# Loading the last row tile of the first x in nine transfers of 64, 14, 2, 12, 4, 10, 6, 8 and 8 partitions instead of seventeen, most of them of five

## The chip, the cores and the metric

The kernel runs on one core of a Trainium2 chip. The metric is the device time in microseconds of one execution; lower is better. Before the change the median is 514.57 us (514.47 to 514.59, 4 runs). "Faster" and "slower" mean by over 2%. In the views PE is TensorE (matmuls), DVE VectorE, ACT ScalarE, POOL GpSimd and SPq the queue of the sync engine; a packet is one record of a DMA engine's work, and a transfer lands when its data has arrived.

## The reference

```
x: (32, 512, 1024) float32     weight: (32, 1024, 768) float32
out = np.matmul(x, weight)     (32, 512, 768) float32
```

Thirty-two independent matrix products. The core must read 168 MB and write 50 MB.

## The kernel before

Weights and x come in through GpSimd's DMA queue, cast to bf16 on the way. The first x alone comes uncast through the sync queue: three row tiles in one transfer, the fourth ("x_fourth", called one_sb in the profile) in pieces:

```
x_first = x_pool.tile([P, MT - 1, K], F32, name="x_sb")
x_fourth = one_pool.tile([P, 1, K], F32, name="one_sb")
nc.sync.dma_start(x_first, x_view[0, :, :MT - 1])
few = [slice(at, first + 20, 4) for first in (0, 20, 40) for at in range(first, first + 4)]
for rows in (slice(64, 96), slice(96, 112), slice(112, P), slice(60, 62), slice(62, 64), *few):
    nc.sync.dma_start(x_fourth[rows, 0], x_view[0, rows, MT - 1])
load_w(0)
```

One partition's row of this tile is 4 KB; "a row" below means one of these. Nothing before the third matmul group of batch 0 needs the tile. At the end of the kernel the sync queue carries the last stores:

```
nc.sync.dma_start(out_view[b - 1, :, halves[0]], outs[b - 1][:, halves[0]])
for late in range(B - LATE, B - 2):
    nc.sync.dma_start(out_view[late], outs[late])
nc.sync.dma_start(out_view[b - 1, :, halves[1]], outs[b - 1][:, halves[1]])
# ... cut: matmuls of the last batch, which issue its two half stores from the sync queue
```

Of the kernel before, what the change touches and what calls it, by code (L numbers as in the profile page):

```python
# [13 lines left out]
def kernel(  # L14
# [9 lines left out]
    P = 128  # L24
# [29 lines left out]
    def banks():  # L54
        return [mpsum.tile([P, 512], F32, name=f"pm{i}") for i in range(3)]

    def load_pair(b):

        xs[b] = x_pool.tile([P, 2 * MT, K], BF16, name="x_sb")
        nc.gpsimd.dma_start(out=xs[b], in_=pair_view[b // 2])  # L60

    def load_last():
        xs[B - 1] = x_pool.tile([P, MT, K], BF16, name="x_sb")
        nc.gpsimd.dma_start(out=xs[B - 1], in_=x_view[B - 1])  # L64

    def load_w(b):
        ws[b] = w_pool.tile([P, KT, N], BF16, name="w_sb")
        at = 0
        for n in CHUNKED.get(b, (KT,)):
            nc.gpsimd.dma_start(out=ws[b][:, at:at + n, :], in_=w_view[b, :, at:at + n, :])  # L70
            at += n
# [9 lines left out]
    def transpose_pair(b, mt):  # L81

        both = xT_pool.tile([P, 2, JT, P // 2, 2, 2], BF16, name="xT")
        for half in range(2):
            nc.vector.tensor_copy(  # L85
                both[:, :, :, :, half, :].rearrange("p b j i r -> p j b i r"),
                words(b, mt + MT * half).rearrange("p j (b i r) -> p j b i r", b=2, r=2),
            )
        return [both[:, r].rearrange("p j i h r -> p j (i h) r") for r in range(2)]

    def transpose_last(mt):
        xT = xT_pool.tile([P, JT, P, 2], BF16, name="xT")
        nc.vector.tensor_copy(  # L93
            xT.rearrange("p j m r -> p (j m r)"), words(B - 1, mt).rearrange("p j m -> p (j m)")
        )
        return xT

    def transpose_first(mt):

        xT = xT_pool.tile([P, JT, P, 2], BF16, name="xT")  # L100
        rows = x_first[:, mt] if mt < MT - 1 else x_fourth[:, 0]
        for h in range(2):
            pt = tpsum.tile([P, JT, P], F32, name="pt")
            for i in range(JT):
                nc.tensor.transpose(pt[:, i, :], rows[:, JT * h + i::KT], ident)  # L105
            nc.vector.tensor_copy(  # L106
                xT[:, 2 * h:2 * h + 2].rearrange("p j m r -> p j r m"),
                pt.rearrange("p (j r) m -> p j r m", r=2),
            )
        return xT  # L110
# [8 lines left out]
    def matmuls(pm, half, xT, b, kos, together):  # L119
        for ko in kos:  # L120
            for i, (bank, at, off, size) in enumerate(SPLITS[half]):
                shares = half == 1 and i == 0
                nc.tensor.matmul(  # L123
                    pm[bank][:, at:at + size],
                    xT[:, ko // 2, :, ko % 2],
                    ws[b][:, ko, off:off + size],
                    start=(ko == 0 and not (together and shares)),
                    stop=(ko == KT - 1),
                    skip_group_check=together,
                )  # L130

    def open_out(b):

        if b == B - 2:
            outs[b] = one_pool.tile([P, MT * N], F32, name="one_sb")
            return
        if b % 2 == 0 or b == B - 1:
            twos[b // 2] = out_pool.tile([P, 2, MT * N], F32, name="out_sb")
        outs[b] = twos[b // 2][:, b % 2]

    def evacuate(b, pair, pm):
        o = outs[b][:, pair * N2:(pair + 1) * N2]
        nc.scalar.copy(o[:, 0:512], pm[0])  # L143
        nc.vector.tensor_copy(o[:, 512:1024], pm[1])  # L144
        nc.scalar.copy(o[:, 1024:N2], pm[2])  # L145

    with tc.manual_schedule():

        x_first = x_pool.tile([P, MT - 1, K], F32, name="x_sb")
        x_fourth = one_pool.tile([P, 1, K], F32, name="one_sb")  # L150
        nc.sync.dma_start(x_first, x_view[0, :, :MT - 1])  # L151
        few = [slice(at, first + 20, 4) for first in (0, 20, 40) for at in range(first, first + 4)]
        for rows in (slice(64, 96), slice(96, 112), slice(112, P), slice(60, 62), slice(62, 64), *few):
            nc.sync.dma_start(x_fourth[rows, 0], x_view[0, rows, MT - 1])
        load_w(0)
        ident = const.tile([P, P], F32)
        make_identity(nc, ident)
        load_pair(1)
        load_w(1)
        load_w(2)  # L160
        load_pair(3)

        def store(at):
            nc.gpsimd.dma_start(out=two_view[at], in_=twos[at])  # L164

        ready = {}
        for b in range(B):
            if b % 2 and b + AHEAD + 1 < B:
                if b + AHEAD + 1 == B - 1:
                    load_last()  # L170
                else:
                    load_pair(b + AHEAD + 1)
            if b % 2 and 2 < b < B - HELD - AHEAD:
                store((b - 3) // 2)
            if b + AHEAD < B:
                load_w(b + AHEAD)
            if b == B - LATE:
                store(b // 2 - 2)
                store(b // 2 - 1)
            if b == B - 1:  # L180
                halves = [slice(pair * N2, (pair + 1) * N2) for pair in range(2)]
# [4 lines that stand above are left out]
            open_out(b)  # L186
            if b == 0:
                xT = {mt: transpose_first(mt) for mt in range(MT - 1)}
            elif b == B - 1:
                xT = {mt: transpose_last(mt) for mt in range(MT)}  # L190
            else:
                if b % 2:
                    for mt in range(MT):
                        ready[b, mt], ready[b + 1, mt] = transpose_pair(b, mt)
                xT = {mt: ready.pop((b, mt)) for mt in range(MT)}
            if b not in CHUNKED:
                for pair in range(2):
                    pm = banks()
                    for half in range(2):
                        mt = 2 * pair + half  # L200
                        if mt not in xT:
                            xT[mt] = transpose_first(mt)
                        matmuls(pm, half, xT[mt], b, range(KT), False)
                    evacuate(b, pair, pm)
                continue
            pms = [banks() for _ in range(2)]
            at = 0
            for n in CHUNKED[b]:
                last = at + n == KT
                for mt in range(MT):  # L210
                    matmuls(pms[mt // 2], mt % 2, xT[mt], b, range(at, at + n), True)
                    if last and mt % 2 == 1:
                        pair = mt // 2
                        evacuate(b, pair, pms[pair])
                        if b == B - 1:
                            nc.sync.dma_start(out_view[b, :, halves[pair]], outs[b][:, halves[pair]])
                at += n
# [30 lines left out]
```

## Time and profile before

| | before |
|---|---|
| time, median | 514.57 us |
| span in the profile | 512.7 us |
| TensorE busy | 435.4 us (85%) |
| memory traffic | 218.1 MB, 425 GB/s |
| x_fourth used from | 42.9 us |
| TensorE's waits for weights | 26.2 us |

Two more lines matter. The first is the group of the main matmuls from the page: busy time and mean duration behind the first bar, the idle time before them and its main cause behind the second. The second is the queue row of the sync engine's transfers, with packets, bytes and share:

```profile
L123 PE MATMUL pm<-w_sb,xT 128*128 128x256 bf16 (+1 forms) x2048 | 353.7, 336 | 26.4 <-DMA w_sb<-in_weight_dram 26.2
q1 hardware_dynamic: 1248, 8.39, 4.1%
```

Below the views lie the packet records of the trace: start, duration, bytes and queue of every DMA packet. They carry no engine number. But every transfer ends with a four-byte completion packet on each engine it used, so a weight load leaves sixteen of them, and an engine's lag against the others can be followed from load to load. Where this text says "the packet records", it means that.

### The profile page before, as it was taken

Reading aid. Unit: us, or ns where it says so; the run is one execution under the profiler, and the core shown is the slowest. Engines: PE = TensorE matmul, PEld = TensorE weight load, DVE = VectorE, ACT = ScalarE, POOL = GpSimd, SP = SyncE. Lnnn points to the kernel's source line nnn. Section 1 sums busy time; section 2 is a strip of 40 time slices with the busy share of each in tenths; the row PEclk is TensorE's granted clock in tenths of the full one; section 3 lists DMA queues with packets and bytes.
Section 4 is the critical chain, followed back from the end, with each engine's and each line's share of the span. In section 5 each row is a group of like instructions: output and inputs, shape, how many; then the busy total and the mean of one; then the engine's idle time right before and its main releaser. Section 6 shows DMA issues by size and latency. Waiting matters only on the chain.

```text
span 512.7 us, 5785 instructions
## 1 busy us (share of the span) xinstructions
PE 435.4 (85%) x2576; PEld 278.7 (54%) x2576; DVE 130.0 (25%) x196; ACT 76.1 (15%) x129; POOL 39.1 (8%) x73
## 2 busy tenths in 40 slices
PE   1806999999999996997989989798898989999991
PEld 1504666666666663654646546464464645666660
DVE  0202324141515141320413205041040410514121
ACT  1100121212121201111111111111101111120201
POOL 3000010101010101001010000101001000010000
PEclk9956999999999998997999989899798998999997
DMA  8999999999999999999999999999999999999998
GB/s 240 224 221 213 218 220 216 333 221 310 243 218 336 215 324 231 228 325 220 330 223 234 318 223 334 217 247 304 221 333 218 258 295 220 331 215 212 320 427 345
DMA packets 12712, 135.63 MB, mean 265 GB/s; under 512 B 1296, under 2 KB 1296, under 8 KB 3088
## 3 DMA queue, kind: packets, MB, share of 16 engines
q0 software_dynamic: 11440, 126.88, 96.6%
q1 hardware_dynamic: 1248, 8.39, 4.1%
q8 instruction: 20, 0.33, 0.2%
q14 instruction: 4, 0.03, 0.0%
HBM read 167.77 MB, written 50.33 MB: 425 GB/s over the span
## 4 chain that ended last, share of the span: by engine, by line
PE 46%; DMA 37%; issue 8%; DVE 5%; another core or an unknown queue 1%; POOL 1%; ACT 0%; SPq 0%; POOLq 0%
PE pm L123 40%; DMA w_sb<-in_weight_dram 28%; DMA one_sb<-in_x_dram 8%; PE pt L78 5%; DVE xT L85 4%; DVE out_sb L144 1%; POOL out_dram L164 0%; PE pt L105 0%; POOL w_sb L70 0%; POOL x_sb L60 0%; DVE one_sb L144 0%; DVE xT L93 0%; ACT out_sb L145 0%; SPq L151 0%
## 5 line engine op out<-in xcount | busy, mean ns | idle before, releaser
L123 PE MATMUL pm<-w_sb,xT 128*128 128x256 bf16 (+1 forms) x2048 | 353.7, 336 | 26.4 <-DMA w_sb<-in_weight_dram 26.2
L123 PEld LDWEIGHTS <-xT 128*128 128x128 bf16 x2048 | 205.3, 101 | 170.3 <-DMA w_sb<-in_weight_dram 29.3
L144 DVE COPY out_sb<-pm 128x512 f32<-128x512 f32 x62 | 42.9, 691 | 317.6 <-PE pm L123 317.6
L78 PE MATMUL pt<-ident,x_sb 128*128 128x128 f32 x496 | 79.8, 302 | 10.5 <-DVE xT L85 10.2
L78 PEld LDWEIGHTS pt<-ident,x_sb 128*128 128x128 f32 x496 | 69.3, 209 | 21.5 <-DVE xT L85 18.7
L85 DVE COPY xT<-pt 128x1024 bf16<-128x1024 bf16 x120 | 77.4, 687 | 11.0 <-PE pt L78 11.0
L143 ACT COPY out_sb<-pm 128x512 f32<-128x512 f32 x62 | 36.3, 585 | 271.7 <-PE pm L123 271.7
L145 ACT COPY out_sb<-pm 128x512 f32<-128x512 f32 x62 | 36.3, 585 | 145.7 <-PE pm L123 145.6
L70 POOL DMA_DIRECT2D w_sb<-in_weight_dram x37 | 20.1, 544 | 404.8 <-PE pm L123 397.6
L105 PE MATMUL pt<-ident,one_sb 128*128 128x128 f32 x8 | 1.9, 421 | 19.1 <-DMA one_sb<-in_x_dram 19.1
L106 DVE CAST xT<-pt 128x512 bf16<-128x512 f32 x8 | 5.8, 733 | 34.6 <-PE pt L105 34.1
L105 PE MATMUL pt<-ident,x_sb 128*128 128x128 f32 x24 | 5.3, 383 | 10.5 <-DMA x_sb<-in_x_dram 10.3
L105 PEld LDWEIGHTS pt<-ident,one_sb 128*128 128x128 f32 x8 | 1.6, 219 | 19.4 <-issue 19.4
L164 POOL DMA_DIRECT2D out_dram<-out_sb x14 | 10.1, 719 | 6.7 <-ACT out_sb L143 3.5
L105 PEld LDWEIGHTS pt<-ident,x_sb 128*128 128x128 f32 x24 | 4.1, 209 | 11.5 <-issue 10.3
L60 POOL DMA_DIRECT2D x_sb<-in_x_dram x15 | 8.1, 539 | 10.9 <-DMA w_sb<-in_weight_dram 10.9
L144 DVE COPY one_sb<-pm 128x512 f32<-128x512 f32 x2 | 1.4, 690 | 9.0 <-PE pm L123 9.0
L93 DVE COPY xT<-pt 128x1024 bf16<-128x1024 bf16 x4 | 2.6, 686 | 0.2 <-PE pt L78 0.2
L143 ACT COPY one_sb<-pm 128x512 f32<-128x512 f32 x2 | 1.2, 585 | 6.4 <-PE pm L123 6.4
L145 ACT COPY one_sb<-pm 128x512 f32<-128x512 f32 x2 | 1.2, 585 | 1.6 <-PE pm L123 1.6
L143 ACT ACT_TABLE_LOAD x1 | 1.3, 1283 | 0.7 <-PEq L232 0.7
L64 POOL DMA_DIRECT2D x_sb<-in_x_dram x1 | 0.5, 528 | 2.1 <-DMA w_sb<-in_weight_dram 2.1
(6 smaller groups left out, 0.9 us busy)
## 6 DMA issues: line engine op xcount, KB each, us to landing
w_sb<-in_weight_dram POOLq DMA_DIRECT2D x28, 1536.0 KB, 41.7
out_dram<-out_sb POOLq DMA_DIRECT2D x14, 3072.0 KB, 55.3
x_sb<-in_x_dram POOLq DMA_DIRECT2D x15, 2048.0 KB, 49.8
w_sb<-in_weight_dram POOLq DMA_DIRECT2D x7, 768.0 KB, 38.2
out_dram<-out_sb SPq DMA_DIRECT2D x2, 1536.0 KB
x_sb<-in_x_dram SPq DMA_DIRECT2D x1, 1536.0 KB
out_dram<-one_sb SPq DMA_DIRECT2D x2, 768.0 KB
out_dram<-out_sb SPq DMA_DIRECT2D x2, 768.0 KB
```

The lines of the kernel that those rows point to most:

```text
L60: nc.gpsimd.dma_start(out=xs[b], in_=pair_view[b // 2])
L70: nc.gpsimd.dma_start(out=ws[b][:, at:at + n, :], in_=w_view[b, :, at:at + n, :])
L78: nc.tensor.transpose(pt[:, j, :], pairs[:, mo, j::JT], ident)
L85: nc.vector.tensor_copy(both[:, :, :, :, half, :].rearrange("p b j i r -> p j b i r"), words(b, mt + MT * half).rearrange("p j (b i r) -> ...
L93: nc.vector.tensor_copy(xT.rearrange("p j m r -> p (j m r)"), words(B - 1, mt).rearrange("p j m -> p (j m)"))
L105: nc.tensor.transpose(pt[:, i, :], rows[:, JT * h + i::KT], ident)
L106: nc.vector.tensor_copy(xT[:, 2 * h:2 * h + 2].rearrange("p j m r -> p j r m"), pt.rearrange("p (j r) m -> p j r m", r=2),)
L123: nc.tensor.matmul(pm[bank][:, at:at + size], xT[:, ko // 2, :, ko % 2], ws[b][:, ko, off:off + size], start=(ko == 0 and not (together an ...
L143: nc.scalar.copy(o[:, 0:512], pm[0])
L144: nc.vector.tensor_copy(o[:, 512:1024], pm[1])
L145: nc.scalar.copy(o[:, 1024:N2], pm[2])
L164: nc.gpsimd.dma_start(out=two_view[at], in_=twos[at])
```

## The change

The intent, as the code shows it: fewer issues, an earlier landing, and the extra rows spread as a ramp over 14 engines instead of piled on five.

```
-        few = [slice(at, first + 20, 4) for first in (0, 20, 40) for at in range(first, first + 4)]
-        for rows in (slice(64, 96), slice(96, 112), slice(112, P), slice(60, 62), slice(62, 64), *few):
+        ramp = []
+        for at, n in enumerate((14, 12, 10, 8)):
+            ramp += [slice(at, at + 4 * n, 4), slice(at + 4 * n, 64, 4)]
+        for rows in (slice(64, P), *ramp):
             nc.sync.dma_start(x_fourth[rows, 0], x_view[0, rows, MT - 1])
```

Nothing else differs.

## The prediction

> **What bounds the kernel now.** I read the head of the page first, then the chain of waits in order of time, then the DMA view of the last 23 us, and at last the trace's DMA packet records (start, duration, bytes, queue) one by one.
>
> The page says that the 16 DMA engines are busy from the second slice to the last, and the memory line says at what rate:
>
> ```profile
> PE   1806999999999996997989989798898989999991
> DMA  8999999999999999999999999999999999999998
> HBM read 167.77 MB, written 50.33 MB: 425 GB/s over the span
> PE 46%; DMA 37%; issue 8%; DVE 5%; another core or an unknown queue 1%; POOL 1%; ACT 0%; SPq 0%; POOLq 0%
> ```
>
> The reader is to see that PE has gaps and DMA has none. 218.1 MB in 512.7 us is all that the kernel does; TensorE is busy 435 us and fits beside it. The chain names PE for 46%, but a chain only follows the last waits. So I looked where the changed transfer stands in it, and at what happens to the gained time:
>
> ```profile
> 1.18 12.13 DMA one_sb<-in_x_dram
> 13.33 15.00 DMA one_sb<-in_x_dram
> 28.35 14.36 DMA one_sb<-in_x_dram
> 42.90 1.94 PE pt L105 x8
> ...
> 155.40 46.68 DMA w_sb<-in_weight_dram
> ...
> 373.89 49.68 DMA w_sb<-in_weight_dram
> 423.62 6.40 PE pm L123 x28
> ```
>
> The fourth row tile of the first x lands at 42.4 us and lets PE go on at 42.9. PE then runs nearly without a gap (101.3 us busy of the 104 between 43 and 147), and from 147 on it waits for weights. A lead won at 43 is therefore handed to waits for weights after 147. The end itself:
>
> ```profile
> 486.86 0.39 SPq L182 DMA_DIRECT2D out_dram<-one_sb  x1
> 487.30 2.31 SPq L184 DMA_DIRECT2D out_dram<-out_sb  x2
> 489.72 1.11 SPq L185 DMA_DIRECT2D out_dram<-one_sb  x1
> 501.16 1.63 SPq L216 DMA_DIRECT2D out_dram<-out_sb  x2
> ```
>
> The last two stores are issued from 501.2 to 502.8. In the packet records the stores ahead of them end only at 505.6 to 507.4, and the last half store completes between 509.33 and 511.41, engine by engine. A backlog of stores stands between PE's end and the kernel's end, some 3 us deep. **The end is the finish of the slowest DMA engine.** The DMA view of 490 to 513 us (40 slices of 0.575 us) shows the engines running out one after the other at its right end:
>
> ```profile
> DMA  8999999998999899989998999899999998842000
> ```
>
> **How unequal the engines are.** Every weight, x and store transfer from GpSimd ends with 16 four-byte completion packets, one per engine. The time between the completions of two successive weight loads is the same on most engines (7.276 us, 8 packets of 0.907 us), so an engine's lag stays until something is added to it, and I can follow each one. Three kinds appear:
> - Five engines take the twelve transfers of five rows. Between 14.4 and 41 us they fall back by 2.06 us against the rest, 0.17 us for each row with its completion packet; two of them take two rows more and stand at about 2.45 us of lag at 50 us, the other three at 2.2 us.
> - Eight others are hit by the instruction queue: 20 packets of 16384 bytes, 0.9 us each, come in turn to these eight and cost each time about 1.1 us. Four get three, four get two.
> - Three get neither.
>
> The final completions, from the first engine, are 0, 0.17, 0.23 (the three with neither), then 0.80 to 1.21, and at the end 1.65, 1.74, 1.76, 1.85, 2.02 and 2.08 us. The last, 2.08, is an instruction engine with three hits. So are all or nearly all of the six late ones; I can't exclude that one at 1.85 or 2.02 is of the five. The mean is 1.14: perfect balance would gain only 0.94 us, 0.18% of the time. That caps the gain.
>
> **What the Trainium skill says.** "DMA: Bandwidth & Descriptors", section "Why a DMA increments its semaphore by 16 and not by 1": a transfer from the sync queue runs on the largest number of engines, up to 16, that divides its row count, and on the lowest-numbered ones. The trace agrees: the first x and the seventeen pieces leave 128 completion packets, 4 x 16 + 2 x 2 + 12 x 5. The same page, "Queues, rings and completion order": each engine takes turns between its queues, packet by packet. It agrees: in the 5-row stage a small row or a completion packet alternates with a 12288-byte weight packet, a pair every 1.98 us. "Runtime: NRT & Kernel Launch", "Instruction fetch mechanics": instructions are refilled in 16 KiB blocks by a queue of their own; the 20 packets of 16384 bytes fit it. No view names an engine, so which numbers the eight have is my assumption: 8 to 15, as 0 to 4 carry the fives.
>
> **The change part by part.** Rows per engine, from the rule above. Before: three 16-engine transfers give 2+1+1 = 4 to all; two pairs give 2 to engines 0 and 1; the fives give 12 to engines 0 to 4. That is 18 on 0 and 1, 16 on 2 to 4, 4 on 5 to 15 (sum 128). After: the 64 rows give 4 to all; 14, 2, 12, 4, 10, 6, 8, 8 give 8 more to engines 0 and 1, 7 to 2 and 3, 6 to 4 and 5, 5 to 6 and 7, 3 to 8 and 9, 2 to 10 and 11, 1 to 12 and 13, none to 14 and 15. Totals 12, 11, 10, 9, 7, 6, 5, 4 for each pair (sum 128). At 0.17 us a row:
> - engines 0 to 4: 5 or 6 rows fewer, 0.85 to 1.0 us earlier. Mostly not on the end.
> - engines 5 to 7: 5 or 6 more, 0.85 to 1.0 us later, from about 0.1 to about 1.1. Off the end.
> - engines 8 to 15: 3, 3, 2, 2, 1, 1, 0, 0 more, up to 0.5 us later. **These set the end.** Only two completion packets of 4 ns fall away there.
> - Transfers: 17 issues become 9, about 8 x 0.66 us less on the sync queue, which has nothing else to do until 487 us. Worth nothing at the end.
> - Landing of the tile: engine 0 had 14 row-and-completion pairs after the large pieces (14.9 to 42.4 us, 1.96 each). It will have eight after the 64 rows (which should end near 14): four at 2.59 us beside the x pair, four at 1.98, so near 32 us, an estimate. PE goes on 10 us sooner, and waits 10 us more for weights later. DMA order is unchanged, and the queue is never empty in between, so the end does not move by it.
>
> Sum: 0 for PE's lead, 0 for issues, and for the end the last of the eight. If the instruction hits begin at engine 8, the one at 2.08 is engine 10 and gets 2 rows: +0.33. Averaged over the other possible starts the later maximum rises by about 0.2 to 0.25. I take +0.2: 514.55 + 0.2 = **514.75 us**.
>
> **The rivals.**
> 1. PE's ten early microseconds count. For it: the chain gives the small tile 8% and PE is in the chain from 424 to 502. Against it: between them PE waited for weights, in pieces of 47 and 50 us in the chain, which come at the DMA's pace, and after PE's end 3 us of backlog remain. If it were right: up to 504.5 us.
> 2. The balance gains: one of the five engines is truly the last, or the eight don't lie where I think, so that the late ones get no rows. For it: a late engine whose lag grows by 0.07 us each time a store passes seems to be one of the five. Against it: it is at most second. Taking it away alone leaves 2.08, so the gain is under 0.1 us: 514.45 to 514.55. The whole balance would make 513.6.
> 3. The instruction fetches come at other times as PE runs earlier, and hit other packets. Single hits cost from 0.93 to 1.32 us in the records, so 0.2 us either way.
> 4. More rows on more engines slow the weights near the start and PE starves. Against it: the same 0.5 MB of the tile moves in both, and the weights' packets keep 0.907 us beside it.
>
> **Range and chances.** From +0.5 (three rows on the slowest engine) and 0.2 of fetch luck, 515.2 at the top; from -0.1 (rival 2) and 0.15 of luck, 514.3 below. The three runs of before lie within 0.11 us, so noise adds little. A change of 2% would be 10 us, eleven times the whole imbalance; only rival 1 comes near, and not over it: faster 0.004, slower 0.004.
>
> **What would show it.** The fourth tile's transposes (line 105, one_sb) start near 32 instead of 42.9; PE's waits for weights grow by about as much; the DMA row stays at nine and the rate at 425 GB/s; the spread of the last completions loses its three early engines but keeps its last one. I am wrong if the last completions move by over half a microsecond, if the last stores no longer queue behind others, or if the eight late engines turn out to be those that lost rows.

## The result, and the profile after

The changed kernel takes **515.12 us** (median of 4 runs, 514.92 to 515.23) against 514.57 (514.47 to 514.59). The ratio is 1.0011, with an interval of 0.9993 to 1.0028: the same, by the 2% rule. Ratios here are the mean time of one kernel's fast runs over that of the other's of the same rounds, so they are not quite the ratio of the medians. Still, all nine timed runs of the changed kernel (four here, five below) are slower than every run of the kernel before beside them, so the half microsecond is real.

The beginning of the chain of waits after the change (start, length, what) shows the earlier landing:

```profile
1.20 14.03 DMA one_sb<-in_x_dram
15.24 15.25 DMA one_sb<-in_x_dram
30.69 1.94 PE pt L105 x8
```

Its matmul group and queue row, which answer to the two quoted of before:

```profile
L123 PE MATMUL pm<-w_sb,xT 128*128 128x256 bf16 (+1 forms) x2000 | 355.0, 337 | 38.4 <-DMA w_sb<-in_weight_dram 35.9
q1 hardware_dynamic: 1216, 8.39, 4.1%
```

Where the lead went shows in windows of 31 to 43, 43 to 147 and 147 to 424 us (length, then busy time and count of each engine, the granted TensorE clock, DMA share, GB/s), before first:

```profile
31.00:43.00 12.00, 0.10 (x1) 0.13 (x2) 0.00 (x0) 0.00 (x0) 0.00 (x0) 0.50 1.04 225
43.00:147.00 104.00, 101.29 (x615) 66.46 (x616) 32.44 (x49) 16.97 (x29) 9.24 (x16) 0.98 1.02 246
147.00:424.00 277.00, 244.65 (x1427) 154.58 (x1426) 71.27 (x108) 42.14 (x72) 20.82 (x37) 0.94 1.02 267
```

```profile
31.00:43.00 12.00, 11.28 (x60) 8.13 (x60) 7.12 (x11) 0.59 (x1) 0.53 (x1) 0.81 1.03 218
43.00:147.00 104.00, 95.52 (x575) 61.22 (x585) 26.03 (x40) 17.58 (x30) 8.71 (x15) 0.98 1.02 246
147.00:424.00 277.00, 240.60 (x1375) 152.36 (x1399) 70.59 (x107) 41.04 (x70) 20.85 (x37) 0.93 1.02 267
```

TensorE does 11.2 us more in the first window, then 5.8 and 4.0 us less in the next two, while DMA moves the same: 246 and 267 GB/s in both kernels. TensorE starts on the tile 12.2 us earlier (42.90 to 30.69) and waits 9.7 us more for weights (26.2 to 35.9). The lead was handed back. (The record lacks 48 of the matmuls, so the idle time is good to a microsecond or two.) The 32 fewer packets of the sync queue, with the same bytes, are the completion packets of eight fewer transfers: 16 + 16 + 2 + 2 + 12 x 5 + 16 = 112 before, 16 + 14 + 2 + 12 + 4 + 10 + 6 + 8 + 8 = 80 after. That agrees with the rule of how many engines a transfer uses (quoted in the prediction), for 14, 12 and 10 too.

The end is where the two kernels differ. These are the sync queue's last issues after the change, then the DMA view of both kernels from 508 to 513 us, before first. It has 40 slices of 0.125 us; a digit is the mean busy share of the 16 engines in tenths:

```profile
488.06 0.36 SPq L184 DMA_DIRECT2D out_dram<-one_sb  x1
488.46 1.72 SPq L186 DMA_DIRECT2D out_dram<-out_sb  x2
490.66 0.43 SPq L187 DMA_DIRECT2D out_dram<-one_sb  x1
502.36 1.63 SPq L218 DMA_DIRECT2D out_dram<-out_sb  x2
```

```profile
DMA  9899798988888878835534231100000000000000
GB/s 442 344 442 492 295 442 344 442 344 344 344 344 344 344 295 344 344 148 246 246 148 197 98 147 49 49 0 0 0 0 0 0 0 0 0 0 0 0 0 0
```

```profile
DMA  9998978875575754542423132222310100000000
GB/s 393 393 393 344 393 295 344 344 295 246 246 295 246 295 246 197 246 197 98 197 98 148 49 147 98 98 98 98 147 49 0 49 0 0 0 0 0 0 0 0
```

Before, the row stays at 0.7 or more up to the 17th slice and is over nine slices (1.1 us) later. After, it falls to 0.5 at the 10th slice, and a few engines go on alone to the 32nd. By the packet records the engines complete the store ahead of the last two only between 504.6 and 508.4 us, after the last issues began, so there is still a queue and TensorE's end does not set the time. The bytes are the same; why the engines run out less evenly is what the experiments are for.

### The profile page after: what moved, and what is told of

The parts are those of the page before. It is cut to its first block, busy times and chain, and to the rows that moved or that the text cites. A ratio compares the mean times of both kernels' runs of the same rounds, so it can differ in the third digit from the quotient of the medians.

```text
span 513.4 us, 5729 instructions
## 1 busy us (share of the span) xinstructions
PE 436.8 (85%) x2528; PEld 279.6 (54%) x2576; DVE 129.9 (25%) x196; ACT 76.3 (15%) x129; POOL 39.1 (8%) x73
## 4 chain that ended last, share of the span: by engine, by line
PE 49%; DMA 34%; issue 5%; DVE 5%; another core or an unknown queue 3%; POOL 1%; ACT 0%; SPq 0%; POOLq 0%
PE pm L123 44%; DMA w_sb<-in_weight_dram 28%; DMA one_sb<-in_x_dram 6%; PE pt L78 5%; DVE xT L85 4%; DVE out_sb L144 1%; PE pt L105 0%; POOL out_dram L166 0%; POOL w_sb L70 0%; POOL x_sb L60 0%; DVE one_sb L144 0%; DVE xT L93 0%; ACT out_sb L145 0%; SPq L151 0%
## 5 line engine op out<-in xcount | busy, mean ns | idle before, releaser
L123 PE MATMUL pm<-w_sb,xT 128*128 128x256 bf16 (+1 forms) x2000 | 355.0, 337 | 38.4 <-DMA w_sb<-in_weight_dram 35.9
L144 DVE COPY out_sb<-pm 128x512 f32<-128x512 f32 x62 | 42.9, 692 | 330.6 <-PE pm L123 330.6
L143 ACT COPY out_sb<-pm 128x512 f32<-128x512 f32 x62 | 36.3, 586 | 284.2 <-PE pm L123 284.2
L145 ACT COPY out_sb<-pm 128x512 f32<-128x512 f32 x62 | 36.3, 586 | 134.4 <-PE pm L123 134.2
L105 PEld LDWEIGHTS pt<-ident,x_sb 128*128 128x128 f32 x24 | 4.2, 211 | 11.2 <-issue 10.2
```

The lines of the kernel that those rows point to most:

```text
L105: nc.tensor.transpose(pt[:, i, :], rows[:, JT * h + i::KT], ident)
L123: nc.tensor.matmul(pm[bank][:, at:at + size], xT[:, ko // 2, :, ko % 2], ws[b][:, ko, off:off + size], start=(ko == 0 and not (together an ...
L143: nc.scalar.copy(o[:, 0:512], pm[0])
L144: nc.vector.tensor_copy(o[:, 512:1024], pm[1])
L145: nc.scalar.copy(o[:, 1024:N2], pm[2])
```

## The experiments

The theory: the time is the finish of the slowest DMA engine. An engine's finish is its equal share of the main traffic, plus 0.17 us for each extra row of x_fourth, plus about 1.1 us for each 16 KB instruction packet that falls on it. The rival reasons are the early landing (TensorE runs ahead and triggers things elsewhere), the single front transfer, the number of odd transfers, and chance.

First, whom the instruction packets hit. In the changed kernel the transfers are nested: only engines 0 to 13 have a completion of the 14-row transfer, only 0 to 11 one of the 12-row transfer, and so on. So the packet records now give each engine's number up to a pair, and engines 4 and 5 are told apart by the fives of the kernel before, which reach 4 only. The eight engines that take the 16 KB packets are, in their turn: **5**, one of 6 and 7, one of 8 and 9, 10 and 11, 12 and 13, and one of 14 and 15. The order of the durations in a turn also tells where the turn begins. The first turn of three traces:

```
before   892 893 938 945 936 967 974 961 ns
after    893 893 948 944 921 975 974 962 ns
sixes    893 893 948 945 936 974 974 961 ns
```

Twenty packets over eight engines give three to the first four of the turn. The prediction had assumed engines 8 to 15. A second assignment of the packets, with every engine held to the same 715 packets of GpSimd's queue, gave the same eight, and in the changed kernel's first trace it gave each engine exactly the rows of the rule. The four with three hits ended there as follows (us), in the order of the turn:

```
rows added   before   after    later by
    6        510.97   512.12   1.15   (engine 5)
    5        511.08   511.85   0.77
    3        511.40   511.81   0.41
    2        511.35   511.74   0.39
```

All four are later, and the more rows an engine got, the later it is. This is one trace of each kernel; the last completion of the other four traces of the changed kernel is up to 0.4 us later still.

**Ten sixes: engine 5 alone.** In the kernel before, the twelve fives become ten transfers of six rows.

```
-        few = [slice(at, first + 20, 4) for first in (0, 20, 40) for at in range(first, first + 4)]
+        few = [slice(at, first + 24, 4) for first in (0, 24) for at in range(first, first + 4)]
+        few += [slice(48, 60, 2), slice(49, 60, 2)]
```

> Ten transfers of six rows in place of twelve of five: engine 5 gets ten rows more, engines 0 to 4 two fewer, nothing else changes. Theory (engine 5 takes three of the instruction fetches and is among the late ones, as the residues in the trace after say): it finishes 10 x 0.17 = 1.7 us later, the end 1.3 to 1.45 us later: 515.85 to 516.05. Rival, which is the prediction's assumption (the fetches are on engines 8 to 15, engine 5 is one of the three that finish first): engine 5 gets from about 0.1 to 1.8 us and the end stays: 514.5 to 514.65.

Measured: 516.05 us median (515.61 to 516.12, 5 runs) against 514.84 for the kernel before on that chip, which was less quiet (514.46 to 515.47, 9 runs). That is 1.2 us more by the medians and 1.15 by the lowest runs. The DMA view of 508 to 513 us, slices of 0.125 us:

```profile
DMA  9899995987959875715333031101010101101000
GB/s 492 344 442 393 442 393 246 393 344 295 442 246 442 344 295 246 295 49 246 147 147 147 0 147 49 49 0 49 0 49 0 49 0 49 49 0 49 0 0 0
```

From the 27th slice on a single engine is at work: 49 GB/s is one packet of 6144 bytes in a slice, and one comes every second slice, as 0.23 us a packet demands. By the packet records that engine completes at 512.82 us and the next at 511.35. It is the one that takes the first, the ninth and the seventeenth instruction packet, and in the trace before it completed at 510.97. Ten rows cost it 1.85 us. So engine 5 is a late engine, and the prediction's assumption falls.

**The early landing alone.** Before's rows per engine, but 25, 25, 5 and 5 rows instead of twelve fives.

```
-        few = [slice(at, first + 20, 4) for first in (0, 20, 40) for at in range(first, first + 4)]
+        few = [slice(0, 50, 2), slice(1, 50, 2), slice(50, 60, 2), slice(51, 60, 2)]
```

> The rows per engine of the kernel before (18, 18, 16, 16, 16, then 4), but the twelve fives become 25, 25, 5 and 5 rows, so that five rows follow each other on an engine and the tile lands early, as it does after the change. Theory (the end is the load of the engine that finishes last): tile at about 34 us instead of 42.4, time as before, 514.5 to 514.65. Rival (the early landing itself costs, because PE runs ahead and its instruction fetches fall elsewhere): at least half of the loss comes too, 514.85 to 515.15.

Measured: 514.53 us median, lowest 514.46; the kernel before on that chip 514.84, lowest 514.46. Two of the five runs were at 515.7, as high as nothing of before went (515.47). The tile is used from 36.3 us. Half of the lead costs nothing that the other three runs show.

**Nearly the whole landing.** The same, with the front in one transfer and four rows in one.

```
-        for rows in (slice(64, 96), slice(96, 112), slice(112, P), slice(60, 62), slice(62, 64), *few):
+        for rows in (slice(64, P), slice(60, 64), *few):
```

> The rest of the early landing: the upper 64 rows in one transfer, then 4, 25, 25, 5 and 5 rows. Engines 0 to 3 carry 17 rows, engine 4 16, all others 4, as before within one row, but the tile lands about as early as after the change, near 31 to 34 us. Theory (load decides, the lead is worth nothing): the lowest times equal, within 0.15 us of before. Rival (the early landing or the single front transfer makes the loss): 0.4 to 0.7 us over before.

**The front alone.** The upper 64 rows in one transfer, all the rest as before.

```
-        for rows in (slice(64, 96), slice(96, 112), slice(112, P), slice(60, 62), slice(62, 64), *few):
+        for rows in (slice(64, P), slice(60, 62), slice(62, 64), *few):
```

> One part of the change alone: the upper 64 rows in one transfer instead of 32, 16 and 16, the pairs and the fives kept. The rows per engine are those of before, two completion packets per engine fewer. Theory: same time within 0.15 us by the lowest runs, landing 1 to 2 us earlier. Rival (this part makes some of the loss): 0.2 us or more over before.

**The changed kernel again**, on the same chip as these two and the next.

> The changed kernel again, unaltered, with the kernel before on one chip. Theory: engines 5, and the next three that take three fetches, get 6, 5, 3 and 2 rows more; engine 5 is the last, its completion near 512.1 us, and the lowest time of the runs is 0.4 to 0.7 us over the lowest of before. If the first difference was chance of the chip: within 0.2.

Measured on this quiet chip, the kernel before at 514.52 us (514.45 to 514.80, 9 runs): nearly the whole landing 514.73 (lowest 514.59), the front alone 514.74 (lowest 514.59), the changed kernel 515.28 (515.19 to 515.64), ratio 1.0013. These are the starts of the tile's transposes in the nearly early kernel, then in the one with the front alone (duration in ns least, median, most; first and last start in us):

```profile
L105 PE MATMUL pt<-ident,one_sb x8: 417/417/449, 33.5 to 35.0; 128*128 128x128 f32 x8
```

```profile
L105 PE MATMUL pt<-ident,one_sb x8: 418/418/451, 41.6 to 43.2; 128*128 128x128 f32 x8
```

One lands 9.4 us early, the other 1.3 us, and both are at 514.7. So the landing makes no difference between them. Both are 0.2 us over before, a little outside what was expected by the medians and inside by the lowest runs. Their packet records show the instruction packets' turn beginning elsewhere, at the fifth and at the third engine of it, which is a likely reason; the runs don't prove it. The changed kernel's 0.76 us is not explained by either part.

**Half the dose.** Six fives and five sixes, so engine 5 gets five rows more. Here and below only the new lines are shown.

```
+        few = [slice(at, first + 20, 4) for first in (0,) for at in range(first, first + 4)]
+        few += [slice(20, 30, 2), slice(21, 30, 2), *[slice(at, 60, 5) for at in range(30, 35)]]
```

> Half the dose of the run with ten sixes: five transfers of six rows and six of five, so engine 5 gets 5 rows more and engines 0 to 4 one fewer. Theory (0.17 us a row on engine 5, which completed at 510.97 in the trace before, the last of all at 511.41): engine 5 completes near 511.85, the end 0.4 to 0.6 us later than before. Rival (any row moved off engines 0 to 4 costs, or sixes cost by their number): half of the 1.2 to 1.5 of the ten sixes, 0.6 to 0.75.

Measured: 514.98 us median (514.64 to 515.33), 0.46 over before. The size fits, but the reason only in part: in its trace the turn began at the seventh engine, so engine 5 (511.66 us) was second, and the last (511.90) was the eighth of the turn, which had three packets this time and no extra row.

**Two rows on engines 5 to 12.** Two transfers of 13 rows, six fives.

```
+        few = [slice(0, 26, 2), slice(1, 26, 2), slice(56, 58), slice(58, 60)]
+        few += [slice(at, 46, 4) for at in range(26, 30)] + [slice(46, 56, 2), slice(47, 56, 2)]
```

> Two transfers of 13 rows put two rows more on each of engines 5 to 12, the fives fall from twelve to six. Theory (each row on a late engine costs 0.17 us at the end, whichever of them it is): 0.34 us over before, 514.85 to 514.95. If only engine 5 counted: it ends at 1.74 + 0.34 = 2.08 after the first, no change, 514.5 to 514.65. If the number of rows on engines 5 to 12 did not count: 514.57 or less.

Measured: 515.25 us median, lowest 515.09, against 514.84 and 514.46 on the less quiet chip: 0.4 to 0.6 more, expected 0.34 (one run was at 516.23). The sign is as expected, but the run does not support the reason: the turn began at the seventh engine here too, and the two last engines of its trace (511.95 and 511.62) are the seventh and the eighth counted from engine 5, with three packets each and no extra row. Those with three packets and two more rows ended at 511.14 and 511.30.

**A better split, tried.** Three rows instead of four for all, the rest on engines 0 to 4.

```
+        few = [slice(0, 25), *[slice(25 + at, 40, 3) for at in range(3)]]
+        few += [slice(40 + at, 64, 6) for at in range(6)] + [slice(at, P, 4) for at in range(112, 116)]
+        for rows in (slice(64, 112), *few):
```

> An attempt at a better split: 48 rows over all 16 engines (3 each instead of 4), 40 in fives (one of 25), 40 in ten fours: 21 rows on engines 0 to 3, 11 on engine 4, 3 on all others. Theory: the late engines end one row (0.17 us) sooner, engines 0 to 3 by 0.5 to 0.85 later but still before them: 514.35 to 514.5. Rival (engines 0 to 3 become the last): 514.6 to 514.9.

Measured: 514.87 us median (514.80 to 514.91), before 514.84 but lowest 514.46. It missed; the rival was right. The packet records name the engine: one of 0 to 3, with 21 rows, which was also hit by two packets of 8192 bytes from another instruction queue, at 135 and 349 us, costing it 0.53 and 0.65 us. It completes last, at 511.66. In the kernel before, as far as the lags can be followed, the same two packets fall on engine 2 or 3, which completes at 511.07 us: at 0.17 us a row it had room for two more rows, and it got five.

**Four more looks**, single runs whose state is therefore unknown, three at the changed kernel and one at the kernel before, to see whether the turn moves from run to run.

> The changed kernel unaltered, one of three looks, to see whether the instruction queue always begins its turn at engine 5. The eight engines tell themselves by the durations of their packets (893, 893, 948, 945, 936, 974, 974, 961 ns, engine 5 first). Theory (late = rows + fetches): a turn that begins at the first or at the seventh of them gives engine 5 three fetches: 515.0 to 515.6. A turn that begins at the third: near 514.95. At the fifth, so that engine 5 gets two: 514.6 to 514.8. Rival (the loss doesn't depend on the fetches): the same time whatever the turn.

> As after_b, the second look at the same kernel. Engine 5 with three fetches: 515.0 to 515.6. With two: 514.6 to 514.95.

> As after_b, the third look at the same kernel. Engine 5 with three fetches: 515.0 to 515.6. With two: 514.6 to 514.95.

> The kernel before unaltered. All eight fetch engines carry 4 rows in it, so the turn should matter less than after the change: 514.4 to 514.9 whatever it is. Rival (before depends on the turn as much): outside of that.

Measured: 515.41, 515.20 and 515.50 us, and 514.66. In all three, as in both earlier traces of the changed kernel, the turn began at engine 5; so did it in both traces of the kernel before, and in the one with ten sixes. These three programs can thus be compared without the turn; in the six others it began elsewhere, and their small differences can't be divided between rows and turn. The turn came with the program and not with the run. What in the program sets it stayed open, and so the wished-for look at the changed kernel with another turn could not be had.

**All fourteen traces together.** For each: the time of the profiled run, the last completion packet of any engine, the mean of the sixteen last completions, and the rank in the turn at which the instruction packets began.

```
kernel           time     last     mean    turn
before          514.44   511.41   510.36   1st
before (b)      514.66   511.62   510.40   1st
front           514.59   511.44   510.40   3rd
early fives     514.53   511.51   510.29   7th
earlier fives   514.84   511.61   510.29   5th
balanced        514.80   511.66   510.12   5th
half sixes      514.98   511.90   510.43   7th
thirteens       515.09   511.95   510.47   7th
after           515.21   512.12   510.11   1st
after (c)       515.20   512.16   510.25   1st
after (b)       515.41   512.36   510.61   1st
after (d)       515.50   512.41   510.23   1st
after (again)   515.64   512.56   510.17   1st
sixes           515.98   512.82   510.29   1st
```

The time is the last completion plus 3.02 to 3.23 us in every one. The mean of the engines lies between 510.1 and 510.6 us and does not follow the time at all: the changed kernel has both the lowest mean and a time 0.8 us over before. **The work is the same; only the worst-loaded engine counts.**

## Why the prediction was right or wrong

The time was right: 515.12 us lies inside 514.3 to 515.2, and the class is the same. That it lies inside is in part luck: in the later rounds the same kernel's median was 515.28. The mechanism was right in kind: the lead is handed back, and the end is the finish of the slowest DMA engine, which extra rows delay. Which engines are late was wrong, and so one term was mis-sized: +0.2 us was forecast for the end and 0.55 came (0.76 in the later rounds). One of the prediction's own signs of being wrong came true: the last completion moved by more than half a microsecond, from 511.41 to 512.12 us.

- *The landing and TensorE's lead.* Near 32 us was forecast, 30.7 came. "Waits 10 us more for weights" was 9.7. The lead was worth nothing, as the two kernels at 514.7 with landings 8 us apart show. Rival 1 falls.
- *The cost of a row.* 0.17 us was read from the trace. In the run with sixes ten rows cost engine 5 1.85 us at the end, 1.67 of it by 65 us as the lags say, so 0.167 a row while they were loaded. In the changed kernel a row cost less, 0.135 to 0.15 us by the lags at 65 us; of engine 5's 1.15 us some 0.8 stood there by then, and the rest, which came later, is not taken apart.
- *The step that failed* is "which numbers the eight have is my assumption: 8 to 15", and with it "engines 5 to 7 ... Off the end". The eight include engine 5, one of 6 and 7, and one of 8 and 9, and the turn begins there. The four with three hits therefore got 6, 5, 3 and 2 rows more, not 3, 3, 2 and 2. Redone with the right numbers: engine 5 completed at 510.97 before; plus 6 x 0.17 is 511.99, which is 0.58 after the last completion of before and gives 515.15 us. It measured 512.12 in the first trace, then 512.16 to 512.56 for the last engine of the other four.
- *A misreading.* "The final completions, from the first engine, are 0, 0.17, 0.23 (the three with neither)": these three packets were the completions of the last store but one on the three slowest engines. A half store takes an engine 1.85 us, less than the spread, so sixteen packets sorted by time are not one transfer's. Followed engine by engine, the three with neither finish at 508.72, 508.72 and 509.13 us, the spread is 2.69 and not 2.08, and perfect balance would be worth 1.05 us, not 0.94. This error did not move the forecast, as it lies at the early end.
- *"So are all or nearly all of the six late ones"* was four of six. The other two are engine 4, which falls back by about 0.07 us once in every two batches, and engine 2 or 3, hit by two 8192-byte packets. The second is what defeated the better split.
- *Rival 2*, a gain by balance, did not come. Its premise did: the eight don't lie where the prediction thought, but the late ones got more rows and not none. *Rival 3* stands as noise: five traces of the changed kernel end between 512.12 and 512.56 us. *Rival 4*: the rate stayed at 425 GB/s.
- *The spread of the last completions* should have lost its three early engines and kept its last one. It grew instead, to 3.82 us: the four with three hits ended later, and the earliest are still the three with neither (508.30, 508.32 and 508.59 us), although two of them got three and five rows more. Rows on an early engine thus did not show at the end; why is open, and the sum "equal share plus rows plus hits" did not hold for these three.

So the change took rows from engines 0 to 4, three of which had room, and gave 16 of these 28 rows to the four that had none. The kernel before, with its odd fives, kept extra rows off every engine above 4. That five was chosen for this is likely, but only argued.

## What to carry to other kernels

Where DMA is busy from end to end, as here, the time is the finish of the worst-loaded engine, and fetches of the program itself are part of its load. A transfer's partition count chooses its engines, so small odd transfers are a lever; but find out which engine is last, by number, before loading any of them, with one run that loads a single engine. And when completions are sorted by time, check that the spread is smaller than one transfer before reading them as one.

## What the Trainium skill lacked or had wrong

- "Runtime: NRT & Kernel Launch", "Instruction fetch mechanics", calls the cost of a 16 KiB boundary "mostly hidden". In these runs the 20 blocks share the engines of the data: each took 0.88 to 0.98 us and set its engine back by about 1.1 us. With all DMA engines busy that was not hidden: four engines carried three of them.
- No page says which engines those blocks use. Here it was eight in turn (5, one of 6 and 7, one of 8 and 9, 10, 11, 12, 13, one of 14 and 15), and the first of the turn was the same in every trace of one program (5 of 5, 2 of 2) and another one in six of the seven other programs.
- No page gives the number, size or cost of the other instruction blocks that come during a run: here four of 8192 bytes, of about 0.32 us each, that cost an engine 0.32 to 0.66 us.
- "DMA: Bandwidth & Descriptors", "Latency and other measured facts", has engines 7 and 15 usually slower. No run here shows these two as slow by themselves: the lag of every late engine that could be followed came from rows, instruction packets or, on engine 4, the small recurring delay.
- Neither lacking nor wrong: the rule for the number of engines on the same page, "Why a DMA increments its semaphore by 16 and not by 1", held for 5, 6, 10, 12, 13, 14 and 25 rows (the last: five engines, and the tile is used from 36.3 us instead of 42.9).
